# A macaron encoder layer in float32 on one core: the first feed-forward block's outgoing products by seven in two groups of six inner chunks, a plain last group of four

## The chip, the cores and the metric

The kernel runs on one core of one Trainium2 chip. The metric is the device time of one launch in microseconds, from all inputs in HBM to the output in HBM; less is better. A time is the median of several executions. The engines are named as the profile does: PE is TensorE's matmul stream and PEld its weight loads, DVE is VectorE, ACT is ScalarE, POOL is GpSimd, SP is SyncE, whose queue issues most of the loads.

## The reference, cut to what matters

One layer is computed for 512 tokens of width 1024, in float32: a gated feed-forward block, a pair of token mixers, and a second feed-forward block, each behind an RMS norm that is shifted and scaled by columns computed from a conditioning vector `c`. The inner width of a feed-forward block is 2816.

```python
def swiglu(h, w_in, w_out):
    gate, up = jnp.split(h @ w_in, 2, axis=-1)
    return (jax.nn.silu(gate) * up) @ w_out

mod = c_act @ w_mod[l] + b_mod[l]
(sh1, sc1, g1, sh2, sc2, g2, sh3, sc3, g3) = jnp.split(mod, N_MOD, axis=-1)

h = modulate(rmsnorm(x, norm_ffn1[l]), sh1, sc1)
x = x + 0.5 * g1[:, None, :] * swiglu(h, w_ffn1_in[l], w_ffn1_out[l])

h = modulate(rmsnorm(x, norm_mix[l]), sh2, sc2)
qa, ka, va, qb, kb, vb, ga, gb = jnp.split(h @ w_in[l], SPLIT_POINTS, axis=-1)
...
x = x + g2[:, None, :] * (merged @ w_out[l])

h = modulate(rmsnorm(x, norm_ffn2[l]), sh3, sc3)
x = x + 0.5 * g3[:, None, :] * swiglu(h, w_ffn2_in[l], w_ffn2_out[l])
```

The change is in the first `swiglu` alone, in its second product (`@ w_out`, here the "outgoing" product), and in what follows it: the update of `x` and the sums of squares for the next norm.

## The kernel before

**Tiling.** Everything is kept transposed: channels on the 128 partitions, the 512 tokens in the free dimension. `x` is eight tiles of 128 x 512. The inner width is 22 chunks of 128; a *unit* is two of them, so units 0 to 10.

**Products.** A float32 product is made of three matmuls on parts: each operand is split by `split_from` into a high part (a cast on ACT) and a low part (a subtraction on DVE), and high x high, high x low and low x high are added up in a PSUM bank. `mm3` (L179 to L181) writes the three at 512 columns (or at 256, for half of the tokens), `two` (L463 to L465) at 256 columns.

**Seven products for eight.** A product of two operands, each cut into 2 x 2 blocks, can be made by seven block products in place of eight, with sums of blocks ahead of them and behind them. The sums of weights are made by DMAs that add to what is in SBUF; these are on POOL's queue. The sums of the moving operand and of the results are DVE instructions. A `Unit` does this: its seven products are s1, a11, a12, s2, s3, s4 and a22. The incoming products of units 3 to 10 are made so (`in_unit1`), 4 deep. Outgoing products are made in *groups* of chunks (`CHUNKS`), in one of two ways:

- *plain* (`Out1`): eight output tiles, each a sum over the group's chunks with three matmuls of 512 columns per chunk, then one update of an `x` tile (L1073, 128 x 512);
- *by seven* (`out_unit1`, the groups numbered in `SEVEN`): two units of seven products, each 3 deep for a group of six chunks, in matmuls of 256 columns. Results are combined by DVE (L543, L548, L551), and `x` is updated in pieces of 128 x 256 (L1001). The moving operand is the gated activation, and `act_split` makes seven pieces of 128 x 256 of it for each of the group's three units: a high and a low of each, and four of the pieces are differences made first. In a plain group the activation of a unit is split by two pieces of 128 x 512.

**The groups before.** Chunks 0 to 5 plain, 6 to 11 by seven, 12 to 15 plain, 16 to 21 plain and last. The last group is special: its first output tiles are made as in any plain group, and the last `LAST_1` of its eight, here four, are made by halves of the tokens, within `boundary`.

**The boundary.** It makes these last tiles for the first half of the tokens, one after the other, then for the second half. Behind each product DVE updates the half tile (L386), ACT squares it (L309), and DVE adds the square to the running sum (L315). When a fixed number of steps (three matmuls each) of the second half has been issued, TensorE adds up the squares of the first half over the channels (L348, into the bank `tp`); DVE and POOL turn that to the norm's factor, and nine steps later TensorE spreads it over the partitions (L337). The numbers are `TO_MIX[0:2]`, 4 and 13. Then DVE and ACT make the hidden state of the first half (L359, L360, L368), and the second half's sums (L348, into `op`) follow the last product. Three gate weights for the mixers are split (L195 `u<-raw,u`) in between.

**Modulation columns.** One of the 9 x 8 columns of `mod` is a load of 512 KB of `w_mod` on SP's queue and one DVE instruction over 128 x 1024 (L288). In the first block 24 of them are made beside the products: each product adds a *rate* to a credit (`side1`), and when this reaches one the next column is asked for, and an earlier one computed.

**The tables.** At the end of the block DVE makes the rotary tables (L1215 to L1245, and L1268 to L1271 for four pairs of tables), two lambda sums (L1251) and a copy of the sink values (L1277). They need one row of parameters that is loaded by `load_row`; this load is issued in the unit two behind the last unit by seven that has a plain unit behind it (the test with `by_sevens`). The first of them (L1215) is tied behind the split that was the last when that load is issued, and all that reads the row behind the last split of the block's weights.

**What sets the order.** A list of items (`items1`) sets TensorE's order of products; `run_items` asks for a weight and splits it a fixed number of items ahead (`ASK`, `MAKE`). On SP and POOL the order is as written. On PE, DVE and ACT a scheduler fixes it when the kernel is built, by its own estimate; within `boundary` it is as written. On the chip each engine then takes its instructions in that order. Buffers are five for raw weights (`RAW`), five pairs of high and low, and PSUM banks: three of `sc`, three of `acc`, one of `op`, one of `tp`.

## Time and profile before

| what | us |
| --- | --- |
| median of 3 timed runs | 1033.41 |
| the runs | 1031.28, 1272.67, 1033.41 |
| the profiled execution | 1030.95 |
| its span in the trace | 1029.2 |
| PE busy | 1023.9 |
| PEld busy | 950.0 |
| DVE busy | 804.4 |
| ACT busy | 593.8 |
| POOL busy | 168.7 |

The profiled execution is one of its own, 1.75 us longer than the span that the trace shows of it. A row of a timeline is the start, the duration, engine, line and operation, the tile written and the tiles read, shapes, and in brackets the idle time before it and who ended it. Durations on one engine overlap a little at their ends, so the cost of an instruction in a busy stretch is the distance of starts. In this execution the outgoing products of the second group are made from about 190 to 226 us, the last group begins at 312.9, its products by halves of the tokens at 332.1.

### The profile page before, as it was taken

The numbers are of one execution on the slowest core, as the hardware profiler recorded it, in microseconds if no ns is written. First come the engines' busy times: TensorE is split into PE (matmuls) and PEld (weight loads), VectorE is DVE, ScalarE is ACT, GpSimd is POOL, SyncE is SP. The second block draws the span as 40 slices with busy tenths as digits, with TensorE's granted clock in tenths as the row PEclk, the third lists the DMA queues.
The fourth block names the chain that finished last, engine by engine and source line by source line (L and its number), as shares of the span: only waits on it lengthen the run. The fifth ranks groups of instructions, "written<-read, shape, count | busy, mean of one in ns | idle before, by whom it ended". The sixth has DMA issues, their size and how long they took to land.

```text
span 1029.2 us, 19174 instructions
## 1 busy us (share of the span) xinstructions
PE 1023.9 (99%) x7454; PEld 950.0 (92%) x7454; DVE 804.4 (78%) x1508; ACT 593.8 (58%) x1040; POOL 168.7 (16%) x197
## 2 busy tenths in 40 slices
PE   9999999999999999999999999999999999999998
PEld 7889899999998988899878888989999999999998
DVE  7887868778878879859772688976898777877877
ACT  6755336553454533768795866534877546655553
POOL 1101011211100100543322101001112112212210
PEclk9999999999999999999999999999999999999999
DMA  9968888998957369696637935974498998999874
GB/s 361 371 192 202 292 220 207 222 227 259 244 153 245 134 259 409 220 274 136 165 83 193 275 120 176 344 243 106 101 237 196 242 231 209 224 223 219 208 156 114
DMA packets 71388, 223.57 MB, mean 217 GB/s; under 512 B 8576, under 2 KB 13312, under 8 KB 71296
## 3 DMA queue, kind: packets, MB, share of 16 engines
q1 hardware_dynamic: 47808, 146.52, 39.4%
q0 software_dynamic: 20352, 71.32, 37.5%
q10 hardware_dynamic: 3136, 4.51, 1.2%
q8 instruction: 58, 0.95, 0.4%
q14 instruction: 34, 0.28, 0.1%
HBM read 212.09 MB, written 10.23 MB: 216 GB/s over the span
## 4 chain that ended last, share of the span: by engine, by line
PE 96%; DVE 2%; ACT 1%; issue 0%; DVEq 0%; ACTq 0%
PE acc L463 7%; PE acc L465 7%; PE acc L464 7%; PE sc L463 7%; PE sc L465 7%; PE sc L464 7%; PE acc L179 5%; PE acc L180 5%; PE acc L181 5%; PE sc L180 4%; PE sc L179 4%; PE sc L181 4%; PE tp L1445 2%; PE sc L192 2%; PE acc L714 2%; PE sc L714 2%
## 5 line engine op out<-in xcount | busy, mean ns | idle before, releaser
L195 ACT CAST high<-raw 128x1024 fp32r<-128x1024 f32 (+2 forms) x176 | 159.0, 914 | 137.7 <-PE acc L464 32.4
L195 DVE TENSOR_TENSOR low<-raw,high 128x1024 fp32r<-128x1024 f32 (+2 forms) x176 | 183.7, 1051 | 42.7 <-ACT high L195 41.7
L463 PE MATMUL acc<-b,high 128*128 128x256 f32 x542 | 150.2, 277 | 0.0
L464 PE MATMUL acc<-b,high 128*128 128x256 f32 x542 | 149.9, 277 | 0.1
L465 PE MATMUL acc<-b,low 128*128 128x256 f32 x542 | 149.9, 277 | 0.0
L464 PE MATMUL sc<-b,high 128*128 128x256 f32 x534 | 147.5, 276 | 0.0
L463 PE MATMUL sc<-b,high 128*128 128x256 f32 x534 | 147.5, 276 | 0.0
L465 PE MATMUL sc<-b,low 128*128 128x256 f32 x534 | 147.5, 276 | 0.0
L195 DVE TENSOR_TENSOR low<-u,high 128x1024 fp32r<-128x1024 f32 (+1 forms) x79 | 93.3, 1181 | 26.7 <-ACT high L195 25.7
L195 ACT CAST high<-u 128x1024 fp32r<-128x1024 f32 (+1 forms) x79 | 80.4, 1019 | 50.0 <-PE sc L464 14.3
L463 PEld LDWEIGHTS acc<-b,high 128*128 128x128 f32 x542 | 101.8, 188 | 0.6 <-DVE f L543 0.3
L464 PEld LDWEIGHTS acc<-b,high 128*128 128x128 f32 x542 | 101.8, 188 | 0.4 <-DVE b L2033 0.3
L465 PEld LDWEIGHTS acc<-b,low 128*128 128x128 f32 x542 | 101.8, 188 | 0.1
L463 PEld LDWEIGHTS sc<-b,high 128*128 128x128 f32 x534 | 100.3, 188 | 0.0
L465 PEld LDWEIGHTS sc<-b,low 128*128 128x128 f32 x534 | 100.3, 188 | 0.0
L464 PEld LDWEIGHTS sc<-b,high 128*128 128x128 f32 x534 | 100.2, 188 | 0.0
L179 PE MATMUL acc<-b,high 128*128 128x512 f32 (+1 forms) x240 | 89.1, 371 | 0.0
L181 PE MATMUL acc<-b,low 128*128 128x512 f32 (+1 forms) x240 | 86.5, 361 | 0.0
L180 PE MATMUL acc<-b,high 128*128 128x512 f32 (+1 forms) x240 | 86.5, 360 | 0.0
L179 PE MATMUL sc<-b,high 128*128 128x512 f32 (+1 forms) x224 | 78.7, 351 | 0.0
L180 PE MATMUL sc<-b,high 128*128 128x512 f32 (+1 forms) x224 | 78.5, 350 | 0.0
L181 PE MATMUL sc<-b,low 128*128 128x512 f32 (+1 forms) x224 | 78.4, 350 | 0.0
(411 smaller groups left out, 2739.1 us busy)
## 6 DMA issues: line engine op xcount, KB each, us to landing
u<-w_mod SPq DMA_DIRECT2D x38, 512.0 KB, 8.4
b<-w_mod SPq DMA_DIRECT2D x32, 512.0 KB, 5.1
raw<-w2i SPq DMA_DIRECT2D x31, 512.0 KB, 5.7
u<-w2i POOLq DMA_DIRECT2D x31, 512.0 KB, 7.0
raw<-w1u SPq DMA_DIRECT2D x24, 512.0 KB, 7.6
u<-w1u POOLq DMA_DIRECT2D x24, 512.0 KB, 8.3
raw<-w_gate SPq DMA_DIRECT2D x16, 512.0 KB, 5.8
low<-w_gate POOLq DMA_DIRECT2D x13, 512.0 KB, 7.2
```

Source lines behind the costliest of these rows:

```text
L179: PE.matmul(out, wh, xh, start=first, stop=False)
L180: PE.matmul(out, wh, xl, start=False, stop=False)
L181: PE.matmul(out, wl, xh, start=False, stop=last)
L192: last = PE.matmul(out, of[j][a], of[j][b], start=i == 0, stop=i == 2).ins
L195: last = S.copy(hi, src), V.tensor_tensor(lo, src, f(hi), ALU.subtract)
L463: PE.matmul(out, wh[:, s], xh, start=first and j == 0, stop=False, skip_group_check=True)
L464: PE.matmul(out, wh[:, s], xl, start=False, stop=False, skip_group_check=True)
L465: PE.matmul(out, wl[:, s], xh, start=False, stop=last and j == 1, skip_group_check=True)
L714: PE.matmul(out1[i][:, r], w[:, i * P : (i + 1) * P], h[:, r], start=first and r.start == 0, stop=last and r.stop == T, skip_group_check=True,
L1445: PE.transpose(tp[:, j * P : (j + 1) * P], src, ident)
```

## The change

The groups are cut anew: the third has six chunks in place of four and is made by seven as the second is, and the last has four in place of six, plain as before. Of the last group's eight output tiles five in place of four are made by halves of the tokens. The numbers of steps in `TO_MIX` stay as they are. The units' rates for columns behind the groups by seven become 0.4 and 0.3 for 0.5 and 0.25, and a new pair `AMONG` gives a rate of 0.15 to the units and the outgoing products of the groups by seven, where it was nothing. The lead `MAKE` of one for a unit's s4, which was given to the unit behind the one group by seven, is given to the unit behind each.

```diff
--- before.py
+++ after.py
@@ -106,11 +106,11 @@
 
 MIX_ASIDES = 0, 0, 0, 0, 0, 0, FIRST, ASIDE
 
-CHUNKS = (range(0, 6), range(6, 12), range(12, 16), range(16, 22))
-PLAIN, LAST_1 = 3, 4
-SEVEN, AHEAD_OF, BEHIND = (1,), (0.75, 0.4), (0.5, 0.25)
+CHUNKS = (range(0, 6), range(6, 12), range(12, 18), range(18, 22))
+PLAIN, LAST_1 = 3, 5
+SEVEN, AHEAD_OF, BEHIND, AMONG = (1, 2), (0.75, 0.4), (0.4, 0.3), (0.15, 0.15)
 
 
 EARLY, NEXT, LATER = 3, 3, 4
@@ -903,7 +903,7 @@
         u.p, u.in_order = p, ("s2", "s4")
         if p - 1 in by_sevens:
             u.in_order = ("s1", "s2", "s3", "s4", "a22")
-            if p not in by_sevens:
+            if 2 * p in [CHUNKS[i].stop for i in SEVEN]:
                 u.MAKE = dict(Unit.MAKE, s4=1)
         if p == PLAIN:
             u.asides = {"s1": FIRST}
@@ -1167,7 +1167,7 @@
 
         for v, nxt in zip(order, order[1:] + [None]):
             if v.p - 1 in by_sevens or v not in units1.values():
-                rate = 0.0, 0.0
+                rate = 0.0, AMONG[v not in units1.values()]
             else:
                 rate = AHEAD_OF if v.p <= by_sevens[0] else BEHIND
             n = rate[1]
```

The order of instructions is moved at three places that the prediction speaks of. The first is DVE behind the last group's first products: `x_78`, `x_79`, `x_80` are the first three tiles of `x`, `low<-raw` the low parts of the weights of later tiles, `f` the sums of squares, `ka` and `mod_91` a modulation column, and `u` the tables' rows. Before:

```order
L1073 SCALAR_TENSOR_TENSOR x_78<-acc_3271,mod_90,x_78 128x512
L195 TENSOR_TENSOR low<-raw_3382,high 128x768
L1073 SCALAR_TENSOR_TENSOR x_79<-acc_3286,mod_90,x_79 128x512
L195 TENSOR_TENSOR low<-raw_3386,high 128x768
L315 TENSOR_TENSOR f_261_3308<-f_261_3308,f_263_3322 128x512
L1073 SCALAR_TENSOR_TENSOR x_80<-acc_3330,mod_90,x_80 128x512
L195 TENSOR_TENSOR low<-raw_3390,high 128x768
L315 TENSOR_TENSOR f_261_3308<-f_261_3308,f_265_3350 128x512
L288 ISA b_80_573,mod_91<-b_80_573,ka_96,par 128x1024
L1268 TENSOR_TENSOR u_275_3419<-u_273_3399,u_205_2314 128x4x32
```

After:

```order
L1073 SCALAR_TENSOR_TENSOR x_78<-acc_3525,mod_90,x_78 128x512
L195 TENSOR_TENSOR low<-raw_3591,high 128x512
L1073 SCALAR_TENSOR_TENSOR x_79<-acc_3534,mod_90,x_79 128x512
L195 TENSOR_TENSOR low<-raw_3595,high 128x512
L315 TENSOR_TENSOR f_273_3548<-f_273_3548,f_274_3560 128x512
L288 ISA b_80_573,mod_91<-b_80_573,ka_96,par 128x1024
L1073 SCALAR_TENSOR_TENSOR x_80<-acc_3565,mod_90,x_80 128x512
L195 TENSOR_TENSOR low<-raw_3599,high 128x512
L1251 ISA f_284_3624,lam_s<-u_264_3372 128x64
```

The updates of tiles, lows and sums stand in the same order with 512 for 768 columns in the lows, one column is among them in both. After, `x_80` is the last tile with an L1073, and the tables follow; before, a fourth, of `x_81`, stood among the tables, four rows further.

The second place is DVE a little later, at the end of the tables and the first half of the tokens in `boundary`: `x_81` to `x_85` are the tiles made by halves, `sc` their banks, `u<-raw` the gate weights. Before:

```order
L1277 COPY sink<-u_205_2314 128x2x4
L386 SCALAR_TENSOR_TENSOR x_82<-sc_3470,mod_90,x_82 128x256
L315 TENSOR_TENSOR f_261_3308<-f_261_3308,f_292_3490 128x256
L386 SCALAR_TENSOR_TENSOR x_83<-sc_3493,mod_90,x_83 128x256
L195 TENSOR_TENSOR u_284_3452<-raw_3450,u_283_3451 128x1024
L315 TENSOR_TENSOR f_261_3308<-f_261_3308,f_294_3513 128x256
L386 SCALAR_TENSOR_TENSOR x_84<-sc_3516,mod_90,x_84 128x256
L195 TENSOR_TENSOR u_287_3458<-raw_3456,u_286_3457 128x1024
L315 TENSOR_TENSOR f_261_3308<-f_261_3308,f_296_3536 128x256
L386 SCALAR_TENSOR_TENSOR x_85<-sc_3539,mod_90,x_85 128x256
L195 TENSOR_TENSOR u_290_3464<-raw_3462,u_289_3463 128x1024
L327 TENSOR_SCALAR sm_3579<-tp_3574 128x2
```

After:

```order
L386 SCALAR_TENSOR_TENSOR x_81<-sc_3678,mod_90,x_81 128x256
L315 TENSOR_TENSOR f_273_3548<-f_273_3548,f_302_3692 128x256
L386 SCALAR_TENSOR_TENSOR x_82<-sc_3695,mod_90,x_82 128x256
L195 TENSOR_TENSOR u_294_3660<-raw_3658,u_293_3659 128x1024
L315 TENSOR_TENSOR f_273_3548<-f_273_3548,f_304_3709 128x256
L386 SCALAR_TENSOR_TENSOR x_83<-sc_3712,mod_90,x_83 128x256
L195 TENSOR_TENSOR u_297_3666<-raw_3664,u_296_3665 128x1024
L315 TENSOR_TENSOR f_273_3548<-f_273_3548,f_306_3726 128x256
L386 SCALAR_TENSOR_TENSOR x_84<-sc_3729,mod_90,x_84 128x256
L195 TENSOR_TENSOR u_300_3672<-raw_3670,u_299_3671 128x1024
L315 TENSOR_TENSOR f_273_3548<-f_273_3548,f_308_3743 128x256
L386 SCALAR_TENSOR_TENSOR x_85<-sc_3746,mod_90,x_85 128x256
```

There are five L386 ahead of L327 in place of four, the first is that of `x_81`, straight behind the last row of the tables (L1277), and the low of the third gate weight stands ahead of the last of them.

The third place is PE at the first half's sums of squares (L348): `sc_3561` and `sc_3762` are the banks of the first tile of the second half of the tokens, `b` the activations, `f` the squares. Before:

```order
L179 MATMUL sc_3561<-b_250_3059,high 128x256
L180 MATMUL sc_3561<-b_250_3059,high 128x256
L181 MATMUL sc_3561<-b_250_3059,low 128x256
L179 MATMUL sc_3561<-b_250_3059,high 128x256
L180 MATMUL sc_3561<-b_250_3059,high 128x256
L181 MATMUL sc_3561<-b_250_3059,low 128x256
L348 MATMUL tp_3574<-ones,f_261_3308 128x2 x2
L348 MATMUL tp_3574<-ones,f_298_3559 128x2 x2
L179 MATMUL sc_3561<-b_256_3235,high 128x256
L180 MATMUL sc_3561<-b_256_3235,high 128x256
L181 MATMUL sc_3561<-b_256_3235,low 128x256
```

After:

```order
L179 MATMUL sc_3762<-b_269_3489,high 128x256
L180 MATMUL sc_3762<-b_269_3489,high 128x256
L181 MATMUL sc_3762<-b_269_3489,low 128x256
L179 MATMUL sc_3762<-b_269_3489,high 128x256
L180 MATMUL sc_3762<-b_269_3489,high 128x256
L181 MATMUL sc_3762<-b_269_3489,low 128x256
L348 MATMUL tp_3775<-ones,f_273_3548 128x2 x2
L348 MATMUL tp_3775<-ones,f_310_3760 128x2 x2
L179 MATMUL sc_3787<-b_263_3367,high 128x256
L180 MATMUL sc_3787<-b_263_3367,high 128x256
L181 MATMUL sc_3787<-b_263_3367,low 128x256
```

The sums stood within that tile's product, with two of its six steps left, and stand now behind the whole of it, which is four steps.

## The prediction

> **What bounds the kernel now.** I read the page first, then TensorE's waits, then the edited stretch by itself.
>
> ```profile
> span 1029.2 us, 19174 instructions
> PE 1023.9 (99%) x7454; PEld 950.0 (92%) x7454; DVE 804.4 (78%) x1508; ACT 593.8 (58%) x1040; POOL 168.7 (16%) x197
> PE 96%; DVE 2%; ACT 1%; issue 0%; DVEq 0%; ACTq 0%
> ```
> ```profile
> PE acc L639 <- DVE sm L645: 0.9, 1, 0.9
> PE tp L348 <- ACT f L309: 0.3, 1, 0.3
> ```
>
> TensorE works all the time, and its two waits together are 1.2 us. So every step less on TensorE is time won, at that step's price, as long as what feeds it keeps up. The second wait is the one to look at: L348 adds up the squares for the norm behind the first block, and it waits in the boundary, the place whose split this change alters.
>
> For the stretch from 140 to 343 us (the groups from the second on, up to the boundary) the table of windows gives this sum:
>
> ```profile
> core 0: us, PE busy (x) PEld busy (x) DVE busy (x) ACT busy (x) POOL busy (x), PEclk, DMA share, GB/s
> ...
> sum 203.00, PE 202.70 PEld 195.49 DVE 162.66 ACT 105.47 POOL 28.45; mean PE 33.78 PEld 32.58 DVE 27.11 ACT 17.58 POOL 4.74
> ```
>
> VectorE has 40 us free there, but over 203 us; whether a particular wait is free is a matter of the place.
>
> **The change part by part: TensorE.** TensorE's timeline, once through products of 256 columns, then through products of 512, then through the first products by token halves:
>
> ```profile
> 307.81 0.28 PE L463 MATMUL acc<-b,high 128*128 128x256 f32 x1
> ...
> 312.90 0.40 PE L179 MATMUL acc<-b,high 128*128 128x512 f32 x1
> ...
> 317.15 0.39 PE L179 MATMUL acc<-b,high 128*128 128x512 f32 x1
> ...
> 331.89 0.40 PE L181 MATMUL acc<-b,low 128*128 128x512 f32 x1
> 332.12 0.29 PE L179 MATMUL sc<-b,high 128*128 128x256 f32 x1
> ...
> 334.29 0.28 PE L179 MATMUL sc<-b,high 128*128 128x256 f32 x1
> ```
>
> From 307.81 to 312.90 there are 45 steps of 256 columns: 0.1131 us each. From 317.15 to 331.89 there are 65 steps of 512: 0.2268 us, twice as much. I count in steps of 256 columns at 0.1133. Before, the third group (4 chunks, plain) costs 8 outputs x 4 chunks x 3 products x 2 = 192 steps and the last (6 chunks) 288: 480. After, the third group (6 chunks, by seven) costs 2 units x 7 products x 3 deep x 2 columns x 3 = 252 and the last (4 chunks) 192: 444. Saved: 36 x 0.1133 = 4.1 us, before any wait.
>
> The price of 256 against 512 is what the saving hangs on. The Trainium skill, "TensorE: Matmul & The Clock Gate", section "Back-to-back issue gap", gives about 81 ns for 128 columns and 131 ns for 512 in a real kernel, by which short products cost more than their share. An estimate from that page, half way between them in columns at about 98 ns for 256, would make 252 short steps cost more than the 108 long and the 36 short ones that they replace, and the change lose some 5 us by its products alone. This case's trace disagrees: 0.1131 against 0.2268.
>
> **VectorE's new work.** Groups by form, from 100 to 360 us:
>
> ```profile
> L195 DVE TENSOR_TENSOR low<-raw,high 128x768 fp32r<-128x768 f32 x24 | 22.9, 954 | 7.8 <-ACT high L195 7.8
> ...
> L195 DVE TENSOR_TENSOR b<-f,b 128x256 fp32r<-128x256 f32 x20 | 7.8, 421 | 1.1 <-ACT b L195 0.9
> L195 DVE TENSOR_TENSOR b<-f,b 128x512 fp32r<-128x512 f32 x10 | 6.8, 687 | 1.6 <-ACT b L195 1.6
> ...
> L195 DVE TENSOR_TENSOR low<-raw,high 128x512 fp32r<-128x512 f32 x8 | 5.4, 688 | 0.4 <-ACT high L195 0.4
> ...
> L1001 DVE SCALAR_TENSOR_TENSOR x<-f,sm,x 128x256 f32<-128x256 f32 x8 | 3.5, 478 | 0.0
> ```
>
> Instructions follow each other some 0.09 us closer than these means. Weight lows: 8 of 512 and 8 of 768 columns become 14 of 768 and 8 of 512, six more at 0.87: 5.2 us. Act operands: three units get 7 lows and 4 differences of 256 columns each, 33 x 0.335 = 11.1, for 6 lows of 512 at 0.60 = 3.6: 7.4. Updates of x: 16 at 0.39 and 6 sums of 512 at 0.60, for 8 of 512 at 0.66: 4.6. Together 17 us more, of the 40 free. The units by seven that run already in the second group have the same mix and no wait of TensorE, so I put new waits inside the third group at nothing. If that cover fails, the nearest low there is needed half a microsecond after it is made, and each lost low costs up to its 0.87 us. The modulation columns (13 in the stretch, before and after) only move: five now lie within the groups by seven, where there were none. Loads and queues are in the second rival.
>
> **The boundary.** This is the term that decides. VectorE's timeline there:
>
> ```profile
> 330.40 1.28 DVE L288 CUSTOM_DVE_ANT_0 b<-b,ka,par 128x1024 f32<-128x1024 f32 x1
> ...
> 331.61 0.29 DVE L1268 TENSOR_TENSOR u<-u,u 128x128 f32<-128x128 f32 x1
> ...
> 332.42 0.74 DVE L1073 SCALAR_TENSOR_TENSOR x<-acc,mod,x 128x512 f32<-128x512 f32 x1
> 333.08 0.28 DVE L1268 TENSOR_TENSOR u<-u,u 128x128 f32<-128x128 f32 x1
> ...
> 333.98 0.68 DVE L315 TENSOR_TENSOR f<-f,f 128x512 f32<-128x512 f32 x1
> 334.58 0.28 DVE L1271 TENSOR_TENSOR u<-u,u 128x128 f32<-128x128 f32 x1
> ...
> 336.47 0.48 DVE L386 SCALAR_TENSOR_TENSOR x<-sc,mod,x 128x256 f32<-128x256 f32 x1
> 337.43 0.43 DVE L315 TENSOR_TENSOR f<-f,f 128x256 f32<-128x256 f32 x1 [0.49 <-ACT f L309]
> 337.77 0.48 DVE L386 SCALAR_TENSOR_TENSOR x<-sc,mod,x 128x256 f32<-128x256 f32 x1
> ...
> 339.85 0.48 DVE L386 SCALAR_TENSOR_TENSOR x<-sc,mod,x 128x256 f32<-128x256 f32 x1
> 340.24 1.22 DVE L195 TENSOR_TENSOR u<-raw,u 128x1024 fp32r<-128x1024 f32 x1
> 341.38 0.42 DVE L315 TENSOR_TENSOR f<-f,f 128x256 f32<-128x256 f32 x1
> 341.71 0.48 DVE L386 SCALAR_TENSOR_TENSOR x<-sc,mod,x 128x256 f32<-128x256 f32 x1
> ```
>
> The first half of the tokens has four updates (L386), and the sums need the square behind the last. TensorE meets them here:
>
> ```profile
> 341.85 0.61 PE L348 MATMUL tp<-ones,f 128*128 128x2 f32 x4
> 342.75 0.61 PE L348 MATMUL tp<-ones,f 128*128 128x2 f32 x4 [0.30 <-ACT f L309]
> ```
>
> It begins the sums at 341.85 and gets the last square at 342.75; less about 0.2 of its own work between, it loses 0.7 us. So VectorE is already late here: from 331.61 to 336.47 the table rows (sixteen L1268 to L1271, the lambda sums L1251 and the sink copy L1277) stand ahead of the first L386 in its fixed order. They take 4.86, less the 0.66 of an L1073 (332.42 to 333.08) and the 0.60 of an L315 (333.98 to 334.58) among them: 3.6 us.
>
> After the change I count from T, the end of the first of the final group's products of 512 columns. The order on VectorE from there to the first L386 is three L1073 at 0.66 (2.0), three lows of 512 at 0.60 (1.8), two L315 at 0.60 (1.2), one column at 1.21 (330.40 to 331.61), and the same 3.6 of table rows: 9.8, and 0.3 for squares that ScalarE has to deliver first. The first L386 starts at T + 10.1. The second, third and fourth follow at the distances above: 1.30, 3.38 and 5.24 behind the first. There is a fifth now, and the third gate weight's low stands ahead of it instead of behind the last update; the step from 339.85 to 341.71, which holds the same three things, is 1.86, so it comes at 7.1. From the last L386 to the sums it is 342.75 - 341.71 = 1.0. The sums can run at T + 18.2.
>
> TensorE has less to do meanwhile. In its order there are 14 steps of 512 behind T (3.2 us), five half products of 12 steps, and of the second half one whole product of 12, because four steps are now all of it and not two thirds: 6 x 12 x 0.1133 = 8.2. It is there at T + 11.4 and stands for 6.8 us, partly already at the fourth half product, which needs a bank that the first L386 frees. Against 0.7 before, that is 6.1 lost. Bounds: nothing, if the table rows were all done before T; 8.3, if the square of ScalarE holds VectorE up by 0.49 ahead of each of the three other updates too, as it does at 337.43 ahead of the second.
>
> The second sums (L348 of op) come later in the same boundary. The VectorE row that ends their squares, and the chain's row for the sums:
>
> ```profile
> 352.40 0.43 DVE L315 TENSOR_TENSOR f<-f,f 128x256 f32<-128x256 f32 x1 [0.54 <-ACT f L309]
> ```
> ```profile
> 353.04 0.45 PE op L348 x4
> ```
>
> VectorE is done at 352.83 and TensorE comes at 353.04: 0.2 in hand, no more. The rate's spreading stays at the thirteenth step of the second half, but the half has 20 steps of three products for 24, so TensorE has 4 x 3 x 0.1133 = 1.4 us less cover: 1.2 lost (bounds 0 and 1.4).
>
> Sum against the profiled execution's 1030.95: - 4.1 + 6.1 + 1.2 = 1034.2. The two nearby timed runs lie 0.3 and 2.5 above that execution; I add 0.8 for it: **1035**, 0.2% above the median of 1033.41.
>
> **The rivals.** *The cover holds.* VectorE reaches the first L386 so early that neither sum waits: 1030.95 - 4.1 - 0.7 = 1026.2, with the same 0.8 1027. For it speaks that VectorE is idle a fifth of the stretch, and that only rows in a fixed order hold it; against it, that the fixed order puts 9.8 us of them behind T where TensorE has 11.4 for these and for the five updates and their splits. It decides once some 7 us of that are out of the way. 0.18.
>
> *The loads come late (slower).* Transfers in the out stage of the present group by seven, 190 to 226 us:
>
> ```profile
> DMA packets 2634, 8.76 MB, mean 243 GB/s; under 512 B 288, under 2 KB 288, under 8 KB 2631
> ...
> q0 software_dynamic: 1335, 4.39, 68.4%
> ...
> b<-w_mod SPq DMA_DIRECT2D x1, 512.0 KB, 10.4
> ...
> u<-row SPq DMA_DIRECT2D x1, 260.0 KB, 8.5
> ```
>
> The queue of accumulating loads alone takes 68% of the transfer time, and the column's 512 KB needed 10.4 us. The second such stage gets four columns of 0.52 MB in place of one and the row of 0.27: 1.3 MB more, at 243 GB/s 5.4 us. If all of it delays weights on SP's queue that TensorE waits for, the time is 1034.2 + 5.4 + 0.8 = 1040.4. Against it: the weights are asked for six to nine items ahead, and the present stage runs at this load without a wait. It decides when a raw weight lands later than the 0.5 to 8 us by which its low is early now. 0.16.
>
> *Short steps at the dearer spacing.* From 332.12 to 334.29 eighteen steps of 256 took 2.17 us, 0.1206 each. If the 252 of the third group ran so, they cost 252 x 0.0073 = 1.8 more: 1036.8. That is this kernel's own form of the page's rule on short products. But those eighteen are the products by halves, written by another line (L179 to L181), and the ones of the kind that is added run at 0.1131. 0.06.
>
> **How the numbers follow.** Forecast 0.60; the rivals 0.18, 0.16 and 0.06. The forecast's own range, by its bounds, is 1031 to 1038. The range 1027.3 to 1040.2 takes half of the first rival and most of the second in. Faster by over 2% (below 1012.7) would need five times the products saved: 0.01. Slower by over 2% (above 1054.1) would need all that is counted here twice and more: 0.02. Within 2%, about what a measurement of this kernel tells from no change: 0.97.
>
> **What would show it.** In the changed trace: steps of L463 to L465 at 0.113 in the third group and no PE wait there; the first L386 about 10 us behind the first of the three final L1073; a PE wait of some 3 us at a bank of sc and more at L348 of tp, 6 to 7 in all; about 1 at L348 of op. It is wrong if TensorE waits for lows or raw loads between the two groups by seven, or if its waits at the boundary are below 2 us.

## The result: 1042.0 us, slower by 1.0%

The changed kernel takes 1042.01 us (median of four runs, 1041.29 to 1045.12) against 1032.35 for the kernel before: a ratio of 1.0103, 95% interval 1.0074 to 1.0133. One of the four runs of the kernel before took 1272.67 and is left out of the ratio; the other three lie at 1031.12 to 1033.41. So the change is slower by more than the noise, and by less than 2%. The forecast was 1035, the range 1027.3 to 1040.2. The profiled execution took 1042.25, 11.3 more than that of the kernel before. Its page:

```profile
span 1040.5 us, 19462 instructions
PE 1030.0 (99%) x7550; PEld 960.4 (92%) x7550; DVE 821.2 (79%) x1557; ACT 604.6 (58%) x1068; POOL 176.3 (17%) x205
PE 90%; DVE 5%; ACT 3%; DMA 1%; issue 1%; POOL 0%; DVEq 0%; SPq 0%; ACTq 0%
```

VectorE's busy time rose by 16.8 us, for the 17 that were worked out. TensorE's busy time rose by 6.1, though it has 36 steps of 256 columns less to do: it is busy for longer on each. Its four longest waits:

```profile
PE sc L179 <- DVE x L386: 3.3, 1, 3.3
PE op L348 <- DVE f L315: 1.3, 1, 1.3
PE acc L639 <- DVE sm L645: 0.9, 1, 0.9
PE acc L463 <- ACT f L541: 0.9, 1, 0.9
```

The first two are those of the boundary, at the places and nearly of the sizes that were forecast. The fourth is new and lies far ahead, at 183 us, in the first group by seven.

To see where the 11.3 us lie I cut the execution at three starts of TensorE: its first product of 256 columns behind 139 us, the first product by halves (L179 in a bank of `sc`), and the second spreading (L337 in `op`). Between the first two, every distance of starts is compared with 0.1133 for 256 columns and 0.2267 for 512: what one step has beyond that by over 0.1 us is counted as a stop, the rest as spacing. "Behind" is counted up to the start of the last product. Where the granted clock is 0.50, steps of 256 columns stand about 0.21 us apart; such steps lie in the first stretch of experiments 2, 7, 9, 10 and 13, and a part of their slowness is counted as stops there.

| us | to the first cut | first stretch | of it stops | of it spacing | boundary | behind |
| --- | --- | --- | --- | --- | --- | --- |
| before | 139.7 | 192.4 | 0.4 | 0.3 | 23.9 | 669.2 |
| changed | 140.4 | 196.8 | 1.6 | 4.8 | 29.4 | 669.9 |
| forecast for changed | 139.7 | 191.1 | 0.4 | 0.3 | 28.5 | 669.2 |

In the forecast's row the boundary is 23.94 + 6.1 + 1.2 for the waits, less 2 x 1.36 for the steps saved there. So the boundary came within 0.9 us of it, and 5.7 us were missed ahead of it: 1.2 of stops, and 4.5 because the steps themselves stand wider apart. The 0.7 ahead and 0.7 behind are within what the experiments' profiles scatter by where they run the same code (139.5 to 140.9, 668.7 to 671.5).

VectorE's row of L548 before, then the timeline of VectorE, ScalarE and TensorE around the new wait in the changed kernel:

```profile
178.62 0.68 DVE L548 TENSOR_TENSOR f<-f,op 128x512 f32<-128x512 f32 x1
```
```profile
179.52 1.22 DVE L288 CUSTOM_DVE_ANT_0 b<-b,ka 128x1024 f32<-128x1024 f32 x1
...
180.66 0.68 DVE L548 TENSOR_TENSOR f<-f,op 128x512 f32<-128x512 f32 x1
```
```profile
181.38 0.64 ACT L883 ACTIVATE f<-f 128x512 f32<-128x512 f32 x1 [2.34 <-DVE f L548]
181.91 0.82 ACT L195 CAST high<-raw 128x768 fp32r<-128x768 f32 x1
182.64 0.58 ACT L541 COPY f<-acc 128x512 f32<-128x512 f32 x1
```
```profile
182.11 0.28 PE L464 MATMUL sc<-b,high 128*128 128x256 f32 x1
183.27 0.39 PE L463 MATMUL acc<-b,high 128*128 128x256 f32 x1 [0.88 <-ACT f L541]
```

A modulation column (L288) stands ahead of L548 on VectorE, and L548 starts 2.0 us later than before, of which 0.8 is that all of this stretch lies later. ScalarE's SiLU (L883) waits for L548, and the copy that empties the bank (L541) stands behind it in ScalarE's order; TensorE needs that bank. Behind this stop the products of 256 columns change their pace. Windows of the changed kernel, of which the first begins at the stop:

```profile
183.00:271.00 88.00, 87.73 (x744) 87.73 (x745) 74.55 (x118) 50.52 (x78) 17.65 (x20) 1.00 0.96 247
299.00:326.00 27.00, 27.00 (x232) 27.00 (x230) 24.64 (x46) 13.12 (x19) 1.75 (x2) 1.00 0.69 194
344.17:351.00 6.83, 6.06 (x28) 6.09 (x29) 6.23 (x12) 4.42 (x7) 0.00 (x0) 0.50 0.49 159
364.65:368.06 3.41, 3.41 (x17) 3.41 (x18) 1.73 (x5) 1.84 (x3) 0.71 (x1) 0.50 0.15 56
```

The columns are PE, PEld, DVE, ACT and POOL busy, the granted clock, DMA share and GB/s. 744 steps in 88 us at a clock of 1.00 are 0.118 us each, not 0.113. The last two rows are the two stretches at the boundary in which the clock itself is at 0.50. The first begins 0.8 us ahead of the end of the boundary's first wait (at 344.94), the second 2.0 us behind the end of its second wait (at 362.64).

### The profile page after: what moved, and what is told of

Read it like the earlier page. It is cut to its first block, busy times and chain, and to the rows that moved or that the text cites. A ratio compares the mean times of both kernels' runs of the same rounds, so it can differ in the third digit from the quotient of the medians.

```text
span 1040.5 us, 19462 instructions
## 1 busy us (share of the span) xinstructions
PE 1030.0 (99%) x7550; PEld 960.4 (92%) x7550; DVE 821.2 (79%) x1557; ACT 604.6 (58%) x1068; POOL 176.3 (17%) x205
## 4 chain that ended last, share of the span: by engine, by line
PE 90%; DVE 5%; ACT 3%; DMA 1%; issue 1%; POOL 0%; DVEq 0%; SPq 0%; ACTq 0%
PE acc L463 7%; PE acc L465 7%; PE acc L464 7%; PE sc L465 7%; PE sc L463 7%; PE sc L464 7%; PE acc L179 4%; PE acc L180 4%; PE acc L181 4%; PE sc L179 3%; PE sc L180 3%; PE sc L181 3%; PE acc L714 2%; PE tp L1445 2%; PE sc L714 2%; PE acc L1367 2%
## 5 line engine op out<-in xcount | busy, mean ns | idle before, releaser
L463 PE MATMUL acc<-b,high 128*128 128x256 f32 x576 | 160.3, 278 | 0.9 <-ACT f L541 0.9
L464 PE MATMUL acc<-b,high 128*128 128x256 f32 x576 | 159.9, 278 | 0.1
L465 PE MATMUL acc<-b,low 128*128 128x256 f32 x576 | 159.9, 278 | 0.0
L463 PE MATMUL sc<-b,high 128*128 128x256 f32 x568 | 157.5, 277 | 0.0
L464 PE MATMUL sc<-b,high 128*128 128x256 f32 x568 | 157.4, 277 | 0.0
L465 PE MATMUL sc<-b,low 128*128 128x256 f32 x568 | 157.4, 277 | 0.0
L195 ACT CAST high<-u 128x1024 fp32r<-128x1024 f32 (+1 forms) x85 | 85.4, 1005 | 45.8 <-PE sc L464 11.3
L463 PEld LDWEIGHTS acc<-b,high 128*128 128x128 f32 x576 | 108.1, 188 | 1.6 <-ACT f L541 1.1
L464 PEld LDWEIGHTS acc<-b,high 128*128 128x128 f32 x576 | 108.6, 189 | 0.3 <-DVE b L2033 0.3
L465 PEld LDWEIGHTS acc<-b,low 128*128 128x128 f32 x576 | 108.2, 188 | 0.1
L464 PEld LDWEIGHTS sc<-b,high 128*128 128x128 f32 x568 | 107.1, 189 | 0.0
L463 PEld LDWEIGHTS sc<-b,high 128*128 128x128 f32 x568 | 106.6, 188 | 0.2 <-ACT f L541 0.2
L179 PE MATMUL acc<-b,high 128*128 128x512 f32 (+1 forms) x228 | 84.1, 370 | 0.0
L180 PE MATMUL acc<-b,high 128*128 128x512 f32 (+1 forms) x228 | 81.8, 359 | 0.0
L179 PE MATMUL sc<-b,high 128*128 128x512 f32 (+1 forms) x184 | 65.4, 356 | 3.3 <-DVE x L386 3.3
L195 ACT CAST b<-f 128x256 fp32r<-128x256 f32 (+1 forms) x117 | 45.7, 423 | 36.5 <-DVE f L892 11.0
L180 PE MATMUL sc<-b,high 128*128 128x512 f32 (+1 forms) x184 | 65.0, 353 | 0.0
```

What stands on the lines that cost most here:

```text
L179: PE.matmul(out, wh, xh, start=first, stop=False)
L180: PE.matmul(out, wh, xl, start=False, stop=False)
L195: last = S.copy(hi, src), V.tensor_tensor(lo, src, f(hi), ALU.subtract)
L463: PE.matmul(out, wh[:, s], xh, start=first and j == 0, stop=False, skip_group_check=True)
L464: PE.matmul(out, wh[:, s], xl, start=False, stop=False, skip_group_check=True)
L465: PE.matmul(out, wl[:, s], xh, start=False, stop=last and j == 1, skip_group_check=True)
```

## The experiments

Three theories were to be told apart for the 5.7 us. A: the columns beside the groups by seven stop TensorE, and a stop leaves it at the wider spacing. B: the wider spacing belongs to the changed program (loads, places of tiles). The rival of both, from the prediction: products by seven ask more of VectorE and the loads than there is. The boundary's own theory, VectorE's fixed order behind T, was tried beside these. The comparisons are of medians; the pieces are cut as above.

| us, one profiled execution | time, median | first stretch | stops | spacing | boundary |
| --- | --- | --- | --- | --- | --- |
| 1 no columns in the first group | 1036.9 | 192.9 | 2.3 | 0.3 | 28.8 |
| 2 tables early | 1045.9 | 200.9 | 9.2 | 1.3 | 29.1 |
| 3 before, with columns among | 1033.0 | 193.3 | 1.3 | 0.3 | 23.4 |
| 4 waits filled | 1040.3 | 194.6 | 1.8 | 2.5 | 30.2 |
| 5 tables on GpSimd | 1043.8 | 194.4 | 1.7 | 2.3 | 35.4 |
| 6 four tiles by halves | 1034.6 | 196.1 | 2.7 | 0.3 | 25.5 |
| 7 four chunks by seven, six last | 1039.5 | 200.4 | 9.4 | 2.0 | 23.9 |
| 8 changed, again | 1041.6 | 196.4 | 2.4 | 3.7 | 28.6 |
| 9 as 7, columns spread | 1043.4 | 201.2 | 9.9 | 2.3 | 23.4 |
| 10 as 7, columns even | 1043.8 | 205.1 | 14.1 | 2.0 | 23.4 |
| 11 as 6, columns spread | 1040.3 | 199.9 | 4.4 | 2.4 | 24.2 |
| 12 changed, no columns | 1036.5 | 191.7 | 1.1 | 0.3 | 28.8 |
| 13 as 7, no columns | 1033.9 | 194.2 | 3.8 | 1.4 | 23.4 |

The kernel before ran beside them at medians of 1031.2 to 1031.9. Each row's pieces are of one execution, which need not be the median one. In 6 and 11 the first stretch holds 2.7 us more of work and the boundary as much less, because one tile more is made whole.

### 1: no columns in the first group by seven

```diff
-                rate = 0.0, AMONG[v not in units1.values()]
+                rate = 0.0, 0.3 if v.p > CHUNKS[SEVEN[0]].stop // 2 else 0.0
```

> The changed kernel, with no modulation columns asked for in the first group by seven (the second group's rate is 0.3 instead of 0.15, so that their number stays). In the changed kernel TensorE stops once in that group, 0.9 us at 182, behind a column (L288 at 179.52) that VectorE takes ahead of L548, and from there to 271 its products of 256 columns start 0.1178 us apart instead of 0.1133. Theory A (the stop sets the spacing): without the column the stop is gone or down to the 0.2 us of the kernel before, the spacing is 0.1133 over 183 to 271, and the time falls by 0.7 + 747 x 0.0045 = 4.1 us, to about 1038. Theory B (the spacing comes with the busier loads or the tiles' places in the changed kernel): the spacing stays at 0.1178, and only 0.7 us are won.

Measured: 1036.92 (ratio to before 1.0052, interval 1.0037 to 1.0067), 5.1 us less than the changed kernel. The stop at 182 is gone, and the same stretch of products:

```profile
183.00:267.00 84.00, 84.00 (x744) 84.00 (x743) 72.25 (x116) 48.42 (x75) 17.08 (x20) 1.00 0.99 249
```

744 steps take 84 us and not 88, at the same clock and a higher DMA share. This speaks for A and against loads as the cause of the spacing. The denser columns in the second group make another stop, though:

```profile
PE acc L463 <- DVE f L543: 1.1, 1, 1.1
```

It is at 322 us, the last unit's a22; ahead of L543 in VectorE's order stand a column (319.49), two rows of the tables and a low.

### 3: the kernel before, with columns among

```diff
-SEVEN, AHEAD_OF, BEHIND = (1,), (0.75, 0.4), (0.5, 0.25)
+SEVEN, AHEAD_OF, BEHIND, AMONG = (1,), (0.75, 0.4), (0.5, 0.25), (0.15, 0.15)
...
-                rate = 0.0, 0.0
+                rate = 0.0, AMONG[v not in units1.values()]
```

> The kernel before with one part of the change alone: rates of 0.15 for modulation columns within its one group by seven, the groups, the boundary and all else as before. Theory A: a stop of TensorE of 0.5 to 1 us in the group by seven, and from there to the next products of 512 columns a spacing of 0.1178: 0.7 + up to 62 us / 0.1178 x 0.0045 = 2.4, together up to 3 us slower, about 1034 to 1035. Theory B: the same stop at most, spacing 0.1133: 0.5 to 1 us slower.

Measured: 1033.03, ratio 1.0015 (1.0004 to 1.0026). The stop is there, of the same size and at the same place, and yet the spacing behind it is the narrow one (549 steps in 62 us, 0.113):

```profile
PE acc L463 <- ACT f L541: 0.9, 1, 0.9
```
```profile
183.00:245.00 62.00, 62.00 (x549) 62.00 (x548) 52.39 (x80) 34.00 (x50) 11.41 (x13) 1.00 0.92 239
```

So a stop does not always widen the spacing, and the median came out 1.5 us slower, between the two theories. The ten times fall apart in two heaps, five at 1030.9 to 1032.1 and five at 1034.0 to 1035.8, while the thirteen of the kernel before beside them lie within 1030.3 to 1032.4 (up to 1033.8 in the other sets). The distance fits the 2.4 us of a wide stretch from the stop to the next products of 512; only one of the ten was profiled, from the lower heap, so that is argued and not shown.

### 8: the changed kernel, again

> The changed kernel itself once more, with a second profile. Theory A, as it stands after the first experiments (a stop of TensorE leaves its short products at a spacing of 0.1133 or 0.1178 by chance, until the next stop): the stops of 0.9 at 182 and 0.2 at 270 and 298 are there again, the stretches at 0.1178 are others than in the first profile, and the times spread over 1037.5 to 1042, by up to 4.4 us. Theory C (the spacing is fixed by the program): 0.1178 from 183 to 271 and from 298 to 326 again, and times within 1 us of 1042.

Measured: 1041.59 (1040.27 to 1045.25). The same program at the same stop is wide again up to 271, but no more from 299 on. And the fourth experiment, which is the same program up to the boundary, has the same stop with the narrow spacing behind it, and becomes wide only at a stop at 270 (0.2 us of wait, 0.4 by the distance of starts). Windows of this run, then of the fourth experiment:

```profile
183.00:271.00 88.00, 88.00 (x748) 88.00 (x749) 74.03 (x118) 50.42 (x77) 17.64 (x20) 1.00 0.96 247
299.00:326.00 27.00, 26.68 (x232) 26.15 (x230) 25.02 (x46) 13.39 (x20) 1.75 (x2) 1.00 0.70 196
```
```profile
184.00:269.00 85.00, 85.00 (x752) 85.00 (x752) 73.69 (x118) 50.30 (x77) 17.61 (x20) 1.00 0.98 256
```

748 steps in 88 us here, 752 in 85 there, with the same clock of 1.00 and nearly the same load on every other engine. (From 299 to 326 the count is the same as in the first profile because a stop of 0.7 us lies in that window; the steps between are at 0.113.) B falls: the spacing is not fixed by the program. Neither theory's times came true, though: A let them fall to 1037.5, C held them within 1 us of 1042, and all nine runs of the changed kernel lie from 1040.27 to 1045.25. The two at 1045 have no profile.

Over the fifteen profiles every wide stretch of more than 20 us that lies in the first stretch, seven of them, begins at a stop (0.2 to 1.2 us), and it ends at another stop or at products of 512 columns; of the stops of that size most leave the spacing narrow. The stop of 0.9 us at 182 is in five profiles; two are wide behind it, and of the ten without it none is wide there.

The second feed-forward block, whose code is the same in all these kernels, has wide stretches of more than 20 us too, one each in experiments 1, 5, 8, 11 and 13: 215 to 364 steps, so 1.0 to 1.6 us at 0.0045 a step. Four of them begin behind a step of 0.16 to 0.52 us; that of experiment 1 begins at 787.2 where no step is longer than 0.12, and all five end among products of 256 columns without a stop. Windows of experiment 1, within its stretch and behind it:

```profile
787.00:811.00 24.00, 24.00 (x206) 24.00 (x206) 21.79 (x36) 16.24 (x26) 5.18 (x6) 1.00 0.88 210
813.00:837.00 24.00, 24.00 (x214) 24.00 (x214) 16.85 (x21) 11.40 (x13) 3.48 (x4) 1.00 0.95 230
```

So a stop is neither needed for the wide spacing nor enough for it. That the stop at 182 is what widened the spacing behind it in the changed kernel is likely and not shown; what decides between the two stays open.

### 2: the tables early

```diff
-            if v.p - 2 in by_sevens and v.p - 1 not in by_sevens and v in units1.values():
-                due.append(-1)
+            if v.p == 7 and v in units1.values():
+                due.insert(0, -1)
...
-    behind = split[1]
+    behind = rows[1]
```

> The changed kernel, with the parameter row loaded at unit 7, as the kernel before has it, and the instructions that read it tied behind the split prepared then, not behind the last one. In VectorE's order all table rows then stand ahead of the first update of the final group. The prediction's boundary theory: 3.6 us less stand behind T, the first L386 starts at T + 6.5 instead of T + 10.0, TensorE waits for a bank of sc for nothing or under 0.5 us, and the time falls by 3 to 3.6 us, to about 1038.5. Rival: VectorE is full ahead of T too, so that the rows only delay other work there, a new wait of 2 to 3 us appears ahead of T, and the time stays within 1 us of 1042.

Measured: 1045.91, worse. Two things took the place of what was moved. An incoming weight in the second group by seven is late (ScalarE waits 8.2 us for a load to a `u` tile, up to 295.76); the likely reason is that the row, loaded at 224, keeps one of the six `u` tiles through that group; and in the 3.6 us set free behind T the scheduler put the gate weights' lows, which had stood between the updates:

```profile
PE tp L463 <- ACT high L195: 3.1, 1, 3.1
PE tp L465 <- DVE low L195: 2.5, 1, 2.5
```
```profile
337.52 0.75 DVE L1073 SCALAR_TENSOR_TENSOR x<-acc,mod,x 128x512 f32<-128x512 f32 x1 [0.26 <-PE acc L181]
...
345.58 2.35 DVE L195 TENSOR_TENSOR u<-raw,u 128x1024 fp32r<-128x1024 f32 x2
347.86 0.47 DVE L386 SCALAR_TENSOR_TENSOR x<-sc,mod,x 128x256 f32<-128x256 f32 x1
```

The first L386 is at T + 10.3. The experiment did not take work away behind T, it exchanged it, so it does not tell the boundary's theories apart; neither the theory's 1038.5 nor the rival's 1042 came out.

### 4: the waits filled

```diff
-            for m, products in parts:
+            for i, (m, products) in enumerate(parts):
+                if i == 3:
+                    for _ in range(2):
+                        run(parts[0][1](bank("acc")[:, 0 : 2 * P], ra))
...
             run(steps, at[2])
+            run(parts[0][1](bank("sc")[:, 0 : 2 * P], ra))
             norm.sums(norm.acc, rb, True, False)
```

> The changed kernel with products that nobody reads put into two waits of the boundary: 24 of 256 columns (2.7 us) ahead of the fourth half product, which waits 3.3 us for its bank, and 12 (1.4 us) ahead of the second sums, which wait 1.3. In the changed kernel the granted clock falls to 0.5 to 0.7 for 6 us behind the first wait and to 0.6 to 0.8 for 6 us behind the second. Theory (the clock falls because TensorE stood still): the clock stays at 1.0 over 340 to 370; behind the first wait this saves nothing, since the sums wait for VectorE anyway, behind the second some 1.5 us; the time is 1 to 1.5 us lower, about 1040.8, though TensorE has more to do. Rival (the clock falls for another reason, or its loss is covered in both places): the time is unchanged or up to 1 us higher.

Measured: 1040.26 (ratio 1.0080, 1.0065 to 1.0095). The time is as forecast by the first theory, but not for its reason: the first stretch has 2.3 us less of wide spacing by chance, and the boundary is 0.7 longer. With the second wait filled the clock there is 1.00 (the changed kernel: 0.50 from 364.65 to 368.06), and steps of 256 take 0.117:

```profile
361.00:368.00 7.00, 7.00 (x60) 6.83 (x59) 5.79 (x17) 4.73 (x10) 1.79 (x3) 1.00 0.19 75
```

But the filling is not shown to have kept it there: the changed kernel's second profile (8) and experiment 12 have the same second wait of 1.3 us unfilled, and the clock behind it is 1.00 too. The first drop of the clock did not vanish but moved: TensorE now waits ahead of the sums (1.6 and 0.3 us), and the clock is at 0.50 from 351.4 to 354.9. So where the clock drops behind the second wait it costs about 0.9 us within the boundary (29.4 against 28.6 in 8) and, worked out from half of the 1.4 us that are left of it, 0.7 behind; behind the first wait it costs nothing in the changed kernel, since VectorE sets the time of the sums; and this filling did not win it back. The sums themselves came at the same distance from T as in the changed kernel (L327 at T + 18.82 and T + 18.81): there VectorE alone decides.

### 5: the tables on GpSimd

```diff
-            V.tensor_tensor(C[:, :, 0:NF], cos_t, g0, ALU.mult)
+            G.tensor_tensor(C[:, :, 0:NF], cos_t, g0, ALU.mult)
...
-            V.scalar_tensor_tensor(R[:, :, 0:NF], sin_t, -1.0, g1, ALU.mult, ALU.mult)
+            G.tensor_tensor(R[:, :, 0:NF], minus_sin, g1, ALU.mult)
```

The other two of each four go to GpSimd as well; the rest is as in 1.

> The kernel of the first experiment (no columns in the first group by seven, 1036.9), with the sixteen table rows made by GpSimd instead of VectorE (the negated sine comes from ScalarE). VectorE's order then has the three gate weights' lows in the freed place, ahead of the first L386 instead of between the L386. The prediction's boundary theory: 3.2 us less on VectorE between T and the sums of squares, but the squares of ScalarE now separate the five L386 by 1.3 us each without work between: 2.0 + 1.8 + 1.2 + 3.4 + 0.4 + 0.3 = 9.1 to the first L386, 4 x 1.3 + 1.0 more to the sums, T + 15.3 for T + 17 in the first experiment. TensorE's waits up to the sums fall from 4.6 to about 3, the time by 1.7 us, to 1035.2. Rival (the waits come from the banks or from the squares, not from what stands on VectorE): no change, 1036.9.

Measured: 1043.79, against 1036.9 for the same kernel with the tables on VectorE. VectorE in the boundary:

```profile
329.24 0.94 DVE L195 TENSOR_TENSOR b<-f,b 128x512 fp32r<-128x512 f32 x1
...
346.39 1.23 DVE L195 TENSOR_TENSOR u<-raw,u 128x1024 fp32r<-128x1024 f32 x1 [5.94 <-ACT u L195]
347.53 0.48 DVE L386 SCALAR_TENSOR_TENSOR x<-sc,mod,x 128x256 f32<-128x256 f32 x1
```
```profile
345.31 1.04 ACT L195 CAST u<-raw 128x1024 fp32r<-128x1024 f32 x1 [7.45 <-DMA table_scr<-u]
```

Again the gate weights' lows went ahead of the updates, and the third one waits for its high part: ScalarE's cast stands for 7.5 us until the copy of a `u` tile to `table_scr` has landed, which GpSimd issues at 338.35, behind the tables it now makes. VectorE stands for 5.9 us with the updates behind it in its order, and TensorE for 9.4. While GpSimd computes, VectorE is also slower (0.94 for a low of 512 columns that takes 0.68 in the changed kernel). The Trainium skill, "Perfetto Trace Analysis", section "Optimizing Scalar/DVE Operations", says that the two share a port and that moving work between them might not help; this trace agrees, by that 0.94 for 0.68. As a test of the boundary it fails for the same reason as 2.

### 6: four tiles by halves

```diff
-PLAIN, LAST_1 = 3, 5
+PLAIN, LAST_1 = 3, 4
```

The rest is as in 1.

> The kernel of the first experiment (1036.9) with four tiles by halves in place of five, as the kernel before has them. From T, VectorE has one more L1073 and L315 (1.3 us), one half update and its square less (1.9), and TensorE 12 steps of 512 more ahead of the sums and one half product of 12 steps of 256 less: it comes at T + 12.7 instead of T + 11.4, the sums at T + 16.6. The wait ahead of the sums falls by 1.8 us, the second wait stays or grows by up to 1.4, since only three steps are left behind the spreading: 1035 to 1036.5. Rival: LAST_1 is not what costs, 1036.9 or more.

Measured: 1034.55 (ratio 1.0026, 1.0016 to 1.0035), 2.4 less than 1, a little more than was expected. First stretch and boundary together take 221.7 us in the first experiment's profile and 221.6 here, with a stop at 321 us that is 0.3 longer here by chance or order; so the profiles locate only some 0.4 of the 2.4 us there. Of the 1.5 us between the two profiled executions 1.2 lie behind the boundary, where experiment 1 has its wide stretch in the second block, which has nothing to do with the number of tiles. What they show is the exchange of waits:

```profile
PE tp L348 <- DVE f L315: 1.7, 1, 1.7
PE sc L179 <- DVE x L386: 1.0, 1, 1.0
```

The wait for a bank falls from 2.7 to 1.0 us, and the second sums no longer wait.

### 7: the last group left at six chunks

```diff
-CHUNKS = (range(0, 6), range(6, 12), range(12, 18), range(18, 22))
-PLAIN, LAST_1 = 3, 5
-SEVEN, AHEAD_OF, BEHIND, AMONG = (1, 2), (0.75, 0.4), (0.4, 0.3), (0.15, 0.15)
+CHUNKS = (range(0, 6), range(6, 12), range(12, 16), range(16, 22))
+PLAIN, LAST_1 = 3, 4
+SEVEN, AHEAD_OF, BEHIND, AMONG = (1, 2), (0.75, 0.4), (0.5, 0.25), (0.15, 0.15)
```

> The kernel before with its third group of four chunks made by seven instead of plain (two units of seven products, 2 deep), the last group of six, four tiles by halves and so the boundary as before; no columns in the first group by seven, a rate of 0.3 in the second. TensorE saves 192 - 168 = 24 steps of 256 columns, 2.7 us. Theory (the second group by seven is worth its steps, and the loss of the change lies in the short last group at the boundary and in the stop at 182): the boundary from the first half product to the second spreading takes 24 us as before, there is no stop of 0.9 at 182, and the time is 1031.5 - 2.7 = 1028.8, up to 1031 if a column beside the second group stops TensorE as it did beside the first (1.1 us at 322 in the first experiment). Rival (products by seven cost VectorE more than it has, wherever they are): 1032 or more.

Measured: 1039.54. The boundary takes 23.94 us, to the hundredth what it takes before (all runs with a last group of six: 23.4 to 23.9; with one of four and five halves: 28.6 to 30.2, the fifth experiment apart). So the boundary's loss is that of the short last group. But the first stretch stops for 9.4 us by the table, of which 6.4 are these waits:

```profile
PE sc L463 <- ACT f L541: 3.0, 1, 3.0
PE acc L463 <- ACT f L541: 2.8, 1, 2.8
PE tp L463 <- ACT high L195: 0.6, 1, 0.6
```
```profile
266.00:290.00 24.00, 17.56 (x141) 16.77 (x140) 20.57 (x34) 10.30 (x14) 5.25 (x6) 0.95 1.05 284
```

Here ScalarE's casts wait for raw weights (2.2 and 1.9 us) with L541 behind them; the DMA share is 1.05. This is the prediction's second rival, late loads, with eight columns loaded between 226 and 290; the kernel before loads eight there as well, beside a plain group, and the changed kernel four.

### 9, 10 and 11: the columns laid otherwise

The ninth and tenth are the seventh with other rates (the ninth shown), the eleventh is the sixth with 0.2 and 0.25 likewise.

```diff
-                rate = 0.0, 0.3 if v.p > CHUNKS[SEVEN[0]].stop // 2 else 0.0
+                rate = 0.0, ((0, 0.2), (0.1, 0.15))[v.p > CHUNKS[SEVEN[0]].stop // 2][v not in units1.values()]
```

> The kernel of the seventh experiment (third group of four chunks by seven, last group of six; 1039.5) with the modulation columns spread otherwise: rates of 0.2 for the outgoing products of the first group by seven and nothing for its units, 0.1 and 0.15 in the second, 0.9 and 0.5 behind. Three columns then stand in VectorE's order within the first group's outgoing products, five between there and the second group's last ones, five behind, none behind T. In the seventh experiment TensorE stops for 3.0, 0.8 and 3.1 us at 268 to 288, behind loads that came late at 0.82 to 1.05 of the transfer time, with eight column loads between 226 and 290. Theory (these loads, not the products by seven, cost the time there): the stops go or fall below 1 us in all, TensorE keeps the 2.7 us of its 24 steps, the boundary stays at 24 us, and the time is 1029 to 1031, faster than the kernel before. Rival (two groups by seven load the transfers too much however the columns lie): stops of 2 us or more remain in the second group, 1033 or more.

> As the ninth, with rates of 0.3 for the outgoing products of the first group by seven, 0.2 and 0.2 in the second group, 0.6 and 0.3 behind: three columns among the first group's outgoing products, five in the second group, five behind. Theory as in the ninth, with the columns of the second group a little denser: 1029 to 1032. Rival: 1033 or more.

> The changed kernel's groups (six chunks by seven, four in the last group) with four tiles by halves and the columns spread: 0.2 for the outgoing products of the first group by seven and nothing for its units, 0.25 and 0.25 in the second group, 0.2 and 0.2 behind. What is left against the kernel before is then the short last group at the boundary: 25.5 us from the first half product to the second spreading as in the sixth experiment, for 23.9. TensorE's steps are 36 less, 4.1 us, of which 2.7 lie within these stretches' difference. Theory: no stop of 0.9 at 182 and none of 1.4 at 322, 1032.5 to 1033.5, still no faster than the kernel before. Rival (the stop at 322 comes with the products, not with the columns): 1034.5 as in the sixth.

Measured: 1043.39, 1043.80 and 1040.30. In the ninth and tenth the rivals came out (1033 or more); the eleventh is worse than its theory and than its rival (1034.5). The longest wait of each:

```profile
PE op L465 <- DVE low L195: 2.6, 2, 1.4
```
```profile
PE acc L463 <- ACT f L541: 7.6, 4, 4.6
```
```profile
PE op L465 <- DVE low L195: 1.7, 1, 1.7
```

With three columns among the first group's outgoing products TensorE stops there for 1.1 to 1.9 us at 208 to 210, with a column on VectorE just ahead; further stops follow at 250 to 331. Each of the three is slower, by about 4 to 6 us, than the experiment whose columns it spreads (7 and 6), and all are slower than the kernel before.

### 12 and 13: without these columns

```diff
+    rest = rest[:11]
+    V.memset(modv[SC2][:, 3:], 0.0)
+    V.memset(modv[SH2], 0.0)
...
-        while small_loads and len(rest) < 20:
+        while small_loads and len(rest) < 7:
```

> The changed kernel with the thirteen modulation columns left out that fall beside its products from 140 us on (no load, no sum; zeros stand in their place, which leaves out a part of the mixers' scale and all of their shift). Theory (the columns beside the groups by seven make the stops, and the stops the wider spacing): from the first product of 256 behind 140 us to the first half product TensorE needs 192.4 - 1.4 = 191.1 us with no stop above 0.3, for 196.8 in the changed kernel; the boundary is still that of the short last group, 28.8 us as in the first experiment, for 23.9 before; 1031.2 - 1.4 + 4.9 = 1034.7 in all. Rival (the products by seven stop TensorE by their own lows and loads): 193 us or more in the first stretch, 1036.5 or more.

> The seventh experiment (third group of four chunks by seven, last group of six; 1039.5) with the same thirteen columns left out. Theory: 192.4 - 2.7 = 189.7 us in the first stretch with no stop above 0.3, the boundary as before or 0.7 shorter: 1031.2 - 2.7 - 0.7 = 1027.8; the steps saved then appear in the time where columns and a short last group are both out of the way. Rival: 191.5 us or more in the first stretch, 1030 or more.

Measured: 1036.45 and 1033.92 (ratios 1.0045, 1.0030 to 1.0060, and 1.0021, 1.0011 to 1.0030). In the twelfth the first stretch takes 191.7 us, for 191.1 by theory A and 193 by the rival: no wait of 0.2 us or more is left in it, and 743 steps take 84 us. The median is 1.8 us above the theory's 1034.7, at the rival's 1036.5; the profiled execution, 1035.28, is the fastest of the four, so for the others it is not shown that the stretch has no stop.

```profile
183.00:267.00 84.00, 84.00 (x743) 84.00 (x743) 66.63 (x103) 49.17 (x76) 16.81 (x20) 1.00 0.94 225
```

So with groups of six chunks the products by seven can keep up, and it is with the columns that TensorE stops. What is left against the kernel before is the boundary, 28.8 for 23.9. In the thirteenth it is the other way about: the boundary is as before, but two units of four chunks by seven stop TensorE without any column:

```profile
PE op L465 <- DVE low L195: 1.4, 1, 1.4
```

There the rival holds. Such products are 12 steps long and not 18, while a low is still to be made for each; that this is the reason is argued, not tested.

## Why the prediction was wrong

**Right: the saving and its price per step.** The 36 steps are gone, and short steps cost half of long ones where they run undisturbed: in the twelfth experiment the first stretch is 0.7 us shorter than before, for 1.36 expected, with 0.7 more of stops.

**Right: the boundary, the term that was to decide.** VectorE there, in the changed kernel:

```profile
334.29 0.75 DVE L1073 SCALAR_TENSOR_TENSOR x<-acc,mod,x 128x512 f32<-128x512 f32 x1 [1.57 <-PE acc L181]
...
344.32 0.47 DVE L386 SCALAR_TENSOR_TENSOR x<-sc,mod,x 128x256 f32<-128x256 f32 x1
...
345.61 0.48 DVE L386 SCALAR_TENSOR_TENSOR x<-sc,mod,x 128x256 f32<-128x256 f32 x1
...
347.69 0.48 DVE L386 SCALAR_TENSOR_TENSOR x<-sc,mod,x 128x256 f32<-128x256 f32 x1
...
349.55 0.48 DVE L386 SCALAR_TENSOR_TENSOR x<-sc,mod,x 128x256 f32<-128x256 f32 x1
...
351.41 0.48 DVE L386 SCALAR_TENSOR_TENSOR x<-sc,mod,x 128x256 f32<-128x256 f32 x1
353.10 0.16 DVE L327 TENSOR_SCALAR sm<-tp 128x2 f32<-128x2 f32 x1 [1.21 <-PE tp L348]
```

The first L386 is at T + 10.03 (forecast 10.1), the others 1.29, 3.37, 5.23 and 7.09 behind it (1.30, 3.38, 5.24, 7.1), and the second sums waited 1.3 (1.2). TensorE's wait of 3.3 at the bank of the fourth half product is the 3 that was named; 3.0 more went into that half product and the next two, which ran at a clock of 0.50 up to 351.0 and so came just in time for the sums. The "6 to 7 in all" were therefore not seen as waits here; where the clock stayed up at first, as in experiments 1 and 12, TensorE waits ahead of the sums too (1.6 and 0.3 us). The boundary lost 0.9 more than forecast, behind the second wait, where the clock was 0.50; in the eighth experiment's profile, where it was 1.00, the boundary took 28.6 us, the forecast's 28.5.

**Wrong: "The modulation columns (13 in the stretch, before and after) only move" and "I put new waits inside the third group at nothing".** This is the step that failed. A column moved is not a column at no cost: it was costed as VectorE's busy time, which has room, and not by the place that it takes in VectorE's order. What the prediction went by, the second group that runs without a wait, was a group with no column in it. The prediction looked for new waits in the third group; the first one came in the second group, whose products the change leaves alone, from a column that the new rates put there. The stretch lost 1.2 us of stops and 4.5 more of wide spacing, most of which begins at that stop. Experiment 1 took the columns out of that group and won 5.1; experiment 12 took all thirteen out and the stretch was as forecast to 0.6. The prediction's own sign, steps at 0.113 in the third group, failed as well: they are 0.118 from 299 to 326.

**Wrong: the third rival.** "Short steps at the dearer spacing" named the right kind of loss, with the wrong condition and extent. It was set aside since the kind of product that is added ran at 0.1131 in the profile, at 1.8 us (0.0073 on each of the third group's 252 steps) and a chance of 0.06. What came was 0.0045 on nearly a thousand steps, old and new products alike, in stretches of up to 90 us that begin at stops: 4.5 us. That a stop of 0.9 us in a trace without waits can be followed by such a loss was not in any of the cases.

**The second rival**, late loads, was sound in itself and did not occur in the changed kernel; it occurred in the seventh experiment, when eight columns in place of four were loaded beside the second group.

**The range** reached to 1040.2 and missed by 1.8. Its upper end was most of the second rival, whose 1040.4 does hold the boundary's loss and 5.4 us ahead of it. The 5.7 us that came ahead of it are nearly as much, for another reason, so that size is luck; the rest of the miss is 0.9 at the boundary and 0.7 at each end.

**Smaller slips**, which decide nothing. The 0.7 us that the first sums are said to lose before is 0.4: the eight matmuls of L348 take 1.37 us there and 0.95 in the changed kernel, where they do not wait. The bounds as given add up to 1027.7 to 1037.4, not to 1031 to 1038. And what the 252 short steps replace is 132 long and 24 short ones, by the groups' sizes, not 108 and 36; the "some 5 us" beside it goes with the right counts.

No version that was tried beats the kernel before. The nearest keep the short last group and make four tiles by halves (6: 1034.55), or leave out work (13: 1033.92). Part of the first's lead over experiment 1 is spacing in the second block.

## What to carry to other kernels

When filler work is moved, find what stands behind it in its engine's order at the new place, and who empties a bank for TensorE behind that; room in the busy time says nothing about it. Evidence that a stage runs without a wait holds for what stood beside it there, and no further. On an engine that never waits, the first wait may cost more than its own length: here one of 0.9 us was followed by 4.5 us of wider spacing in the profiled execution, and by none in others. And when the last stage of a block is shortened, count the work of the other engines that its products used to cover: the boundary grew by 5 us here, though 2.7 of the 4.1 us of products saved lie in it.
